# Low parts of the gated branches made by GpSimd and VectorE in turns

## Chip, cores and metric

The kernel runs on one core of a Trainium2 chip. The metric is the device time of one execution, in microseconds (us).

The engines are named as in the profile: PE is TensorE (PEld its weight loads), DVE is VectorE, ACT is ScalarE, POOL is GpSimd, SP issues most of the DMAs.

## The reference

Two layers of a diffusion trunk with two parallel token mixers: neighbourhood attention (branch a) and grouped-query attention (branch b), over 512 latent tokens and 256 context tokens of width 1024. What matters here is the end of a layer. The attention output of each branch is multiplied by the SiLU of its own gate path, projected to width 1024, merged by sigmoid gates, and projected once more:

```python
def _merge(a_att, b_att, a_z, b_z, g_a, g_b, w_o_a, w_o_b, w_out):
    o_a = (a_att * jax.nn.silu(a_z)) @ w_o_a      # width 512 -> 1024
    o_b = (b_att * jax.nn.silu(b_z)) @ w_o_b
    merged = jax.nn.sigmoid(g_a) * o_a + jax.nn.sigmoid(g_b) * o_b
    return merged @ w_out

# _layer:
out_x = _merge(a_att, b_att, a_z, b_z, g_a, g_b, w_o_a, w_o_b, w_out)
x_new = x + gate_x * out_x
```

Layer 0 does this for the context tokens too (768 columns in all), layer 1 for the latent tokens alone (512 columns). Everything is float32.

## The kernel before

**Split products.** A float32 matrix product is made of three matmuls (`mm3`, L435 to L437): both operands are split into a high part, rounded to the matmul's input type, and a low part, the rest; the three are high by high (L435), one with the low part of the activations or weights (L436), and the other (L437). Making a high part is a cast on ACT, making a low part is a subtraction of two SBUF operands. For the weights of the output projections this is L420 and L422 (`load_w2`), for other weights L405 and L408. Their subtractions are shared out by `mix_lo`, which gives odd pieces to DVE and even ones to POOL.

**Gated branches.** The gated outputs of the two branches lie in `za` and `zb`, with channels on partitions: four blocks of 128 channels (f = 0 to 3), each 128 x 768 in layer 0 and 128 x 512 in layer 1. `hilo` makes their high parts (`gah`, `gbh`, casts on ACT, L665) and their low parts (`gal`, `gbl`, subtractions, L666). It is called in three places:
- `prepare()` for all four blocks of branch a. This is in the middle of the grouped-query attention, since the first output projection of branch a (`o_chunks("a", ...)`) is one of the pieces of work with which that stage fills TensorE.
- `early()` for blocks 0 to 2 of branch b, at the end of the grouped-query attention.
- After the attention's pools are closed, block 3 of branch b, with DVE named as the engine.

**Work around them.** In the grouped-query stage each head has four query blocks. For each, TensorE makes scores (`pss`, L884 and L885), DVE subtracts the maximum (L1147), ACT takes the exponential (L1148), DVE or POOL makes the low half of the fp16 split (L836) before the transposing DMA, and TensorE forms the values (L1164, L1165). `divide` (L845 to L848) takes the reciprocal of the row sums, lets TensorE transpose it (L847, into `pst` or `psv`) and multiplies it into `zb` (L848). `head_out` adds the two halves of the value product (ACT L822, DVE L823) and multiplies them into `zb` (L827, on POOL mostly). The queries of the next heads are staged by L878. The context queries of layer 0 have a shorter path (L897, L899, L903).

**The psf bank.** The scores have two PSUM tiles in this stage, and the projections that fill it have one bank, `psf`: one group of twelve matmuls (four blocks by three) must be evicted (L701, DVE, which multiplies by the gate held in `tg`) before the next group may start.

**Order.** The program is not scheduled by hand: a scheduler with a timeline of its own sorts the instructions of each engine into one queue, which the engine then runs in order. An edit of one instruction's engine thus moves others.

The function edited and its callers:

Of the kernel before, what the change touches and what calls it, by code (L numbers as in the profile page):

```python
# [12 lines left out]
ALU = mybir.AluOpType  # L13
# [39 lines left out]
def R(ap):  # L53
    return ap.bitcast(F32R)
# [18 lines left out]
def hybrid_kernel(es: ExitStack, tc, x, ctx, cvec, w_ada, w_ada0, small, gvec, w_in, w_o_a, w_o_b, w_out,  # L73
                  bias_int, bias_edge, rope, ident_d, out):
    nc = tc.nc
    V, S, G, T = nc.vector, nc.scalar, nc.gpsimd, nc.tensor
# [351 lines left out]
    mix_lo = lambda k: V if k % 2 == 1 else G  # L428
# [164 lines left out]
    def layer(l, hx, nxt, start):  # L593
        first = l == 0
        ntok = NTOK if first else NLAT
# [62 lines left out]
        def hilo_tiles(name):  # L658
            return [big(name + part).rearrange("p (f n) -> p f n", f=4) for part in "hl"]

        def hilo(src, dst, fs, lo_eng=G, parts=((0, ntok),)):
            sv = src.rearrange("p (f n) -> p f n", f=4)
            for n0, n1 in parts:
                for f in fs:
                    S.copy(R(dst[0][:, f, n0:n1]), sv[:, f, n0:n1])  # L665
                    lo_eng.tensor_tensor(R(dst[1][:, f, n0:n1]), sv[:, f, n0:n1], dst[0][:, f, n0:n1], ALU.subtract)  # L666

        def load_tg(c):
            nc.sync.dma_start(tg[c].rearrange("p (f n) -> p f n", f=4)[:, :, :ntok], gs[c][:, :, :ntok])
# [18 lines left out]
        def prepare():  # L688

            gated["a"] = hilo_tiles("ga")  # L690
            hilo(za, gated["a"], range(4))
            for c in (0, 2):
                tg[c] = big("tg")
                load_tg(c)
# [90 lines left out]
        if True:  # L785
# [395 lines left out]
            def early():  # L1181

                for c in (1, 3):
                    tg[c] = big("tg")
                    load_tg(c)
                gated["b"] = hilo_tiles("gb")
                hilo(zb, gated["b"], range(3))
# [6 lines left out]
        with tc.tile_pool(name=f"mrg{l}", bufs=1, reuse_waits="tile") as mp:  # L1194
# [3 lines left out]
            for v in range(nv):  # L1198
                src = gd[l][8 * v:8 * v + 8].rearrange("k p -> (k p)").unsqueeze(0)
                nc.sync.dma_start(gv[:, v, :], src.to_broadcast([128, DM]))  # L1200
            hilo(zb, gated["b"], [3], V, spans)
            mg = []

# [312 lines left out]
```

## Time and profile before

| | |
|---|---|
| time, median of 3 runs | 1115.7 us (1115.24 to 1117.81) |
| time of the profiled execution | 1117.27 us |
| its span, first to last instruction | 1115.5 us |
| mean granted TensorE clock | 0.991 |
| busy: PE / DVE / ACT / POOL | 97% / 69% / 55% / 42% |
| L666 on POOL | 8 for branch a, 6 for branch b |
| L666 on DVE | 3, all of block 3 of branch b |

A profile line of the timeline reads: start, duration (both us), engine, line, operation, output tile <- input tiles, shape of output and input, count, and in brackets the idle time ahead of it with what ended it. A line of the waits reads: who waited <- for whom: us in total, times, longest. Where several like instructions follow each other they stand in one row with their count and the time from the first start to the last end.

### The profile page before, as it was taken

Reading aid. Unit: us, or ns where it says so; the run is one execution under the profiler, and the core shown is the slowest. Engines: PE = TensorE matmul, PEld = TensorE weight load, DVE = VectorE, ACT = ScalarE, POOL = GpSimd, SP = SyncE. Lnnn points to the kernel's source line nnn. Section 1 sums busy time; section 2 is a strip of 40 time slices with the busy share of each in tenths; the row PEclk is TensorE's granted clock in tenths of the full one; section 3 lists DMA queues with packets and bytes.
Section 4 is the critical chain, followed back from the end, with each engine's and each line's share of the span. In section 5 each row is a group of like instructions: output and inputs, shape, how many; then the busy total and the mean of one; then the engine's idle time right before and its main releaser. Section 6 shows DMA issues by size and latency. Waiting matters only on the chain. (4 is left out here: it accounts for less than half of the span.)

```text
span 1115.5 us, 16945 instructions
## 1 busy us (share of the span) xinstructions
PE 1077.0 (97%) x5672; PEld 878.7 (79%) x5672; DVE 764.8 (69%) x1600; ACT 617.7 (55%) x1236; POOL 468.2 (42%) x397
## 2 busy tenths in 40 slices
PE   8999999899999999869999999999999899999998
PEld 5688888788888877757788788888877888777677
DVE  4667799974378478676577785467997565677473
ACT  6454279776333576655330284445898446776430
POOL 1054235554246245454421445232446373564531
PEclk9999999999999999979999999999999999999999
DMA  9455324554543597869524542453565436879642
GB/s 370 143 171 151 90 70 115 123 137 121 174 145 110 140 207 172 171 197 261 181 89 133 181 128 79 138 161 98 129 148 133 145 99 169 198 226 238 192 150 78
DMA packets 236000, 171.79 MB, mean 154 GB/s; under 512 B 160140, under 2 KB 201864, under 8 KB 234248
## 3 DMA queue, kind: packets, MB, share of 16 engines
q1 hardware_dynamic: 228576, 156.31, 51.4%
q0 software_dynamic: 2368, 7.87, 2.2%
q10 hardware_dynamic: 4968, 6.53, 1.7%
q8 instruction: 45, 0.74, 0.3%
q14 instruction: 43, 0.35, 0.1%
HBM read 115.58 MB, written 17.32 MB: 119 GB/s over the span
## 5 line engine op out<-in xcount | busy, mean ns | idle before, releaser
L836 POOL TENSOR_TENSOR h<-p,h 128x256 f16<-128x256 f32 (+2 forms) x104 | 113.0, 1095 | 169.0 <-ACT h L835 121.1
L422 POOL TENSOR_TENSOR wlo<-raw,whi 128x512 fp32r<-128x512 f32 x70 | 98.6, 1413 | 124.4 <-ACT whi L420 81.4
L435 PE MATMUL psf<-hx,whi 128*128 128x512 f32 (+1 forms) x360 | 137.5, 382 | 2.5 <-ACT zt L623 1.3
L437 PE MATMUL psf<-hx,wlo 128*128 128x512 f32 (+1 forms) x360 | 135.5, 376 | 0.0
L436 PE MATMUL psf<-hx,whi 128*128 128x512 f32 (+1 forms) x360 | 135.3, 376 | 0.0
L435 PE MATMUL psx<-whi,hx 128*128 128x512 f32 (+1 forms) x328 | 121.0, 372 | 0.0
L420 ACT CAST whi<-raw 128x512 fp32r<-128x512 f32 x136 | 82.9, 620 | 67.9 <-DMA raw<-in_w_in_dram 41.7
L437 PE MATMUL psx<-whi,hx 128*128 128x512 f32 (+1 forms) x328 | 120.0, 367 | 0.0
L436 PE MATMUL psx<-wlo,hx 128*128 128x512 f32 (+1 forms) x328 | 119.6, 366 | 0.0
L405 ACT CAST whi<-raw 128x512 fp32r<-128x512 f32 x88 | 54.4, 623 | 103.9 <-PE psx L437 34.2
L408 POOL TENSOR_TENSOR wlo<-raw,whi 128x512 fp32r<-128x512 f32 x40 | 59.6, 1493 | 122.0 <-ACT whi L405 78.9
L506 POOL TENSOR_TENSOR ss<-ss,ehalf 128x8 f32<-128x8 f32 (+2 forms) x40 | 62.8, 1572 | 82.3 <-DVE ss L503 77.0
L422 DVE TENSOR_TENSOR wlo<-raw,whi 128x512 fp32r<-128x512 f32 x66 | 69.5, 1053 | 35.0 <-ACT whi L420 33.6
L835 ACT CAST h<-p 128x256 f16<-128x256 f32 (+2 forms) x136 | 81.6, 616 | 6.9 <-DMA ct<-h 3.4
L435 PEld LDWEIGHTS psf<-hx,whi 128*128 128x128 f32 x360 | 67.8, 188 | 15.1 <-ACT zt L623 2.4
L1147 DVE CUSTOM_DVE_ANT_0 p<-pss,vb 128x768 f32<-128x768 f32 x64 | 60.3, 953 | 25.7 <-PE pss L885 23.2
L1148 ACT ACTIVATE p<-pss,mx 128x768 f32<-128x768 f32 x64 | 57.6, 900 | 35.8 <-DVE mx L1147 34.9
L437 PEld LDWEIGHTS psf<-hx,wlo 128*128 128x128 f32 x360 | 67.8, 188 | 11.7
L436 PEld LDWEIGHTS psf<-hx,whi 128*128 128x128 f32 x360 | 67.9, 189 | 10.8
L437 PEld LDWEIGHTS psx<-whi,hx 128*128 128x128 f32 x328 | 61.9, 189 | 10.3
L436 PEld LDWEIGHTS psx<-wlo,hx 128*128 128x128 f32 x328 | 62.0, 189 | 9.4
L435 PEld LDWEIGHTS psx<-whi,hx 128*128 128x128 f32 x328 | 61.8, 189 | 9.1 <-issue 0.2
(338 smaller groups left out, 2975.5 us busy)
## 6 DMA issues: line engine op xcount, KB each, us to landing
raw<-in_w_in_dram SPq DMA_DIRECT2D x168, 256.0 KB, 3.0
rawb<-in_w_ada_dram SPq DMA_DIRECT2D x48, 256.0 KB, 2.7
raw<-in_w_out_dram SPq DMA_DIRECT2D x32, 256.0 KB, 2.9
tg<-gs SPq DMA_DIRECT2D x4, 1536.0 KB, 7.1
rawx<-in_w_ada_dram SPq DMA_DIRECT2D x4, 1024.0 KB, 9.8
rawy<-in_w_ada_dram SPq DMA_DIRECT2D x4, 1024.0 KB, 9.8
gs<-zt ACTq DMA_DIRECT2D x16, 256.0 KB, 2.8
raw<-in_w_o_a_dram SPq DMA_DIRECT2D x16, 256.0 KB, 3.2
```

Source lines behind the costliest of these rows:

```text
L405: S.copy(hi[:, :n], raw[:, :n])
L408: e.tensor_tensor(lo[:, :n], raw[:, :n], F(hi[:, :n]), ALU.subtract)
L420: S.copy(hi, raw)
L422: lo_eng(i).tensor_tensor(lo, raw, F(hi), ALU.subtract)
L435: T.matmul(ps, lhs[0], rhs[0], start=first, stop=False)
L436: T.matmul(ps, lhs[0], rhs[1], start=False, stop=False)
L437: T.matmul(ps, lhs[1], rhs[0], start=False, stop=last)
L506: G.tensor_tensor(ss, ss, ehalf[:, :n], ALU.pow)
L835: S.copy(h[:, 0], p[:, :n])
L836: eng.tensor_tensor(h[:, 1], p[:, :n], h[:, 0], ALU.subtract)
L1147: V.tensor_tensor_reduce(p, pss, lift, -1.0, 3e38, ALU.add, ALU.min, mx[:, 0:1])
L1148: S.activation(p, pss, AF.Exp, bias=mx[:, 0:1], accum_out=r[:, i:i + 1])
```

## The change

The default engine of `hilo` is no longer GpSimd. Where no engine is named, block f goes to the engine that `mix_lo` gives for it: blocks 1 and 3 to VectorE, blocks 0 and 2 to GpSimd. The call that names VectorE is not touched. So in each layer f = 1 and 3 of branch a and f = 1 of branch b move to VectorE.

```diff
-        def hilo(src, dst, fs, lo_eng=G, parts=((0, ntok),)):
+        def hilo(src, dst, fs, lo_eng=None, parts=((0, ntok),)):
             sv = src.rearrange("p (f n) -> p f n", f=4)
             for n0, n1 in parts:
                 for f in fs:
                     S.copy(R(dst[0][:, f, n0:n1]), sv[:, f, n0:n1])
-                    lo_eng.tensor_tensor(R(dst[1][:, f, n0:n1]), sv[:, f, n0:n1], dst[0][:, f, n0:n1], ALU.subtract)
+                    (lo_eng or mix_lo(f)).tensor_tensor(R(dst[1][:, f, n0:n1]), sv[:, f, n0:n1], dst[0][:, f, n0:n1], ALU.subtract)
```

The order of the queues changes with it. First VectorE in layer 0, where branch a is prepared; `gal` is the low part, `wlo` a weight's low part, `qs` the staged queries, `mx` and `p` the softmax's. Before:

```order
L897 TENSOR_REDUCE mx_5427<-pss_5422 128x2
L899 TENSOR_SCALAR mx_5427<-mx_5427 128x2
L1147 ISA p_5553,mx_5554<-pss_5548,vb_3419 128x768
L1147 ISA mx_5554 128x1
L848 TENSOR_SCALAR zb_4067<-pst_5616,vb_3419,zb_4067 64x512
L422 TENSOR_TENSOR wlo_5499<-raw_5495,whi_5497 128x512
L878 TENSOR_TENSOR qs_5721<-qb_3734,qs_5721 64x768
L845 RECIPROCAL r_5431<-r_5431 128x2
L823 TENSOR_TENSOR ho_5471<-psv_5462,ho_5471 64x256
```

And now:

```order
L897 TENSOR_REDUCE mx_5427<-pss_5422 128x2
L666 TENSOR_TENSOR gal_5309<-za_1053,gah_5308 128x768
L899 TENSOR_SCALAR mx_5427<-mx_5427 128x2
L848 TENSOR_SCALAR zb_4067<-pst_5616,vb_3419,zb_4067 64x512
L1147 ISA p_5553,mx_5554<-pss_5548,vb_3419 128x768
L1147 ISA mx_5554 128x1
L666 TENSOR_TENSOR gal_5309<-za_1053,gah_5308 128x768
L422 TENSOR_TENSOR wlo_5499<-raw_5495,whi_5497 128x512
L878 TENSOR_TENSOR qs_5721<-qb_3734,qs_5721 64x768
L823 TENSOR_TENSOR ho_5471<-psv_5462,ho_5471 64x256
L845 RECIPROCAL r_5431<-r_5431 128x2
```

Two low parts stand ahead of L422 and of L823, the first (f = 1) also ahead of L899; on GpSimd four in a row have become two at the same place.

TensorE at the same place, where `psf_5322` is the first group of the projection of branch a and `psv_5640` the transposed reciprocals. Before:

```order
L435 MATMUL psf_5322<-gah_5308,whi_5053 128x512
L884 MATMUL pss_5561<-gk_3421,qs_5543 128x512
L885 MATMUL pss_5561<-gk_3421,qs_5543 128x512
L884 MATMUL pss_5561<-gk_3421,qs_5543 128x256
L885 MATMUL pss_5561<-gk_3421,qs_5543 128x256
L847 MATMUL psv_5640<-ident,r_5431 128x128 x2
L884 MATMUL pss_5574<-gk_3421,qs_5543 128x512
```

And now:

```order
L436 MATMUL psf_5322<-gal_5309,whi_5053 128x512
L437 MATMUL psf_5322<-gah_5308,wlo_5055 128x512
L435 MATMUL psf_5322<-gah_5308,whi_5059 128x512
L884 MATMUL pss_5561<-gk_3421,qs_5543 128x512
L885 MATMUL pss_5561<-gk_3421,qs_5543 128x512
L884 MATMUL pss_5561<-gk_3421,qs_5543 128x256
L885 MATMUL pss_5561<-gk_3421,qs_5543 128x256
L884 MATMUL pss_5574<-gk_3421,qs_5543 128x512
L885 MATMUL pss_5574<-gk_3421,qs_5543 128x512
L884 MATMUL pss_5574<-gk_3421,qs_5543 128x256
L885 MATMUL pss_5574<-gk_3421,qs_5543 128x256
L847 MATMUL psv_5640<-ident,r_5431 128x128 x2
```

Three more matmuls of the group (with block 1's low part) and the second score group have moved ahead of L847; the rest of `psf_5322` stands behind it and is now followed by the next group, `psf_5336`, without scores between.

VectorE in layer 1, where branch b is prepared; `psf_10927` is the group of branch a's projection whose eviction (L701) frees the psf bank:

```order
 L823 TENSOR_TENSOR ho_10895<-pst_10882,ho_10895 64x512
+L666 TENSOR_TENSOR gbl_10946<-zb_9765,gbh_10945 128x512
 L701 TENSOR_SCALAR tg_10560<-tg_10560,psf_10927 128x512
 L848 TENSOR_SCALAR zb_9765<-pst_10953,vb_9238,zb_9765 64x512
 L422 TENSOR_TENSOR wlo_11106<-raw_11102,whi_11104 128x512
+L408 TENSOR_TENSOR wlo_11194<-raw_11190,whi_11192 128x512
 L823 TENSOR_TENSOR ho_10973<-pst_10960,ho_10973 64x512
 L827 TENSOR_TENSOR zb_9765<-zb_9765,ho_10973 64x512
-L408 TENSOR_TENSOR wlo_11194<-raw_11190,whi_11192 128x512
 L666 TENSOR_TENSOR gbl_10946<-zb_9765,gbh_10945 128x512
```

Block 1's low part has come between L823 and the eviction L701; the last L666, of block 3, was on VectorE before too. In the same layer the two low parts of branch a go behind L836 and ahead of an L1147, and elsewhere in layer 0 weights' low parts and SP's loads change places with their neighbours.

## The prediction

> **What bounds the kernel now.** I read the page first, then the windows, TensorE's waits, and the timelines of the places where the changed instructions stand.
>
> ```profile
> PE 1077.0 (97%) x5672; PEld 878.7 (79%) x5672; DVE 764.8 (69%) x1600; ACT 617.7 (55%) x1236; POOL 468.2 (42%) x397
> PEclk9999999999999999979999999999999999999999
> ```
>
> TensorE is busy for 97% of the span. An edit on VectorE or GpSimd can therefore win only TensorE's idle gaps and the time in which its clock is lowered, and it loses whatever new gap it makes. The slices show one weak place, the 18th of forty (474 to 502 us), where the granted clock drops to 7 tenths. The windows give its size (start:end, length, then the busy time of each engine, clock, DMA share, GB/s):
>
> ```profile
> 480.00:500.00 20.00, 11.63 (x53) 9.30 (x52) 16.20 (x14) 10.77 (x21) 14.29 (x10) 0.68 0.69 213
> ```
>
> TensorE is busy for 11.63 of 20 us there, at a clock of 0.68. The waits of TensorE name what ended its gaps; the first three rows are of 470 to 640 us (layer 0), the last two of 980 to 1115 us (layer 1):
>
> ```profile
> PE psv L847 <- DVE ho L823: 6.2, 1, 6.2
> PE psf L435 <- ACT zt L623: 1.6, 1, 1.6
> PE psf L436 <- POOL gal L666: 0.6, 1, 0.6
> ...
> PE psf L436 <- POOL wlo L408: 1.7, 1, 1.7
> PE psf L436 <- POOL gbl L666: 1.1, 1, 1.1
> ```
>
> The low parts that are edited (L666) show up as 0.6 and 1.1 us. The 6.2 us stand in VectorE's name, and its timeline shows that this too goes back to L666 on GpSimd. GpSimd first, then VectorE:
>
> ```profile
> 482.29 1.29 POOL L827 TENSOR_TENSOR zb<-zb,ho 64x512 f32<-64x512 f32 x1
> 483.54 1.27 POOL L422 TENSOR_TENSOR wlo<-raw,whi 128x512 fp32r<-128x512 f32 x1
> 484.77 7.14 POOL L666 TENSOR_TENSOR gal<-za,gah 128x768 fp32r<-128x768 f32 x4
> 491.86 1.27 POOL L422 TENSOR_TENSOR wlo<-raw,whi 128x512 fp32r<-128x512 f32 x1
> ```
>
> ```profile
> 483.12 0.56 DVE L899 TENSOR_SCALAR mx<-mx 128x2 f32<-128x2 f32 x1
> 483.67 0.96 DVE L1147 CUSTOM_DVE_ANT_0 p<-pss,vb 128x768 f32<-128x768 f32 x1
> ...
> 484.67 0.76 DVE L848 SCALAR_TENSOR_TENSOR zb<-pst,vb,zb 64x512 f32<-64x512 f32 x1
> 485.45 8.22 DVE L422 TENSOR_TENSOR wlo<-raw,whi 128x512 fp32r<-128x512 f32 x1
> 493.71 0.95 DVE L878 TENSOR_TENSOR qs<-qb,qs 64x768 fp32r<-64x768 f32 x1
> 494.69 0.17 DVE L845 RECIPROCAL r<-r 128x2 f32<-128x2 f32 x1
> 494.89 0.42 DVE L823 TENSOR_TENSOR ho<-psv,ho 64x256 f32<-64x256 f32 x1
> ```
>
> VectorE's subtraction L422, two operands in SBUF, took 8.22 us and ended just after GpSimd's last instruction did (491.86 + 1.27 = 493.13). It did nothing for five GpSimd instructions. Behind it in VectorE's queue stood L823, which frees the bank into which TensorE's L847 writes:
>
> ```profile
> 486.64 0.50 PE L436 MATMUL psf<-gal,whi 128*128 128x512 f32 x1 [0.58 <-POOL gal L666]
> ...
> 487.69 0.63 PE L884 MATMUL pss<-gk,qs 128*128 128x512 f32 x1
> 488.12 0.63 PE L885 MATMUL pss<-gk,qs 128*128 128x512 f32 x1
> ...
> 495.36 0.69 PE L847 MATMUL psv<-ident,r 128*128 128x128 f32 x2 [6.19 <-DVE ho L823]
> ...
> 497.98 0.63 PE L435 MATMUL psf<-gah,whi 128*128 128x512 f32 x1
> 498.41 0.63 PE L436 MATMUL psf<-gal,whi 128*128 128x512 f32 x1
> ...
> 500.89 0.39 PE L885 MATMUL pss<-gk,qs 128*128 128x512 f32 x1
> ...
> 1042.65 0.40 PE L435 MATMUL psf<-gbh,whi 128*128 128x512 f32 x1
> 1042.88 0.39 PE L436 MATMUL psx<-gbl,whi 128*128 128x512 f32 x1
> ```
>
> The starts of neighbouring 128x512 matmuls are 0.43 us apart at 487.69 and at 497.98, and 0.23 at 1042.65: half rate from before the long wait until past 498.4. At 500.89 a matmul takes 0.39 us again. The gaps of 1.6 and 0.6 us, the second of which ended at 486.64, are all that stands in the rows ahead of it. [...]
>
> **The change part by part.** Six of the fourteen low parts that GpSimd makes go to VectorE, three in each layer.
>
> ```profile
> L666 POOL TENSOR_TENSOR gal<-za,gah x8: 1269/1762/1832, 484.8 to 994.7; 128x768 fp32r<-128x768 f32 x4, 128x512 fp32r<-128x512 f32 x4
> L666 DVE TENSOR_TENSOR gbl<-zb,gbh x3: 426/684/1754, 546.4 to 1054.0; 128x512 fp32r<-128x512 f32 x2, 128x256 fp32r<-128x256 f32 x1
> ...
> 543.71 2.23 DVE L422 TENSOR_TENSOR wlo<-raw,whi 128x512 fp32r<-128x512 f32 x1
> ...
> 543.09 6.80 POOL L666 TENSOR_TENSOR gbl<-zb,gbh 128x768 fp32r<-128x768 f32 x3
> ```
>
> A 128x768 low costs GpSimd 7.14 / 4 = 1.79 us, and VectorE 0.95 by the 64x768 subtraction at 493.71 (as many elements for each partition). A 128x512 low takes VectorE 0.68. GpSimd loses about 3 x 1.8 + 3 x 1.4 = 9.6 us (1.4 lies between the row's least, 1.27, and its median), and VectorE gains 3 x 0.95 + 3 x 0.68 = 4.9. Neither sum is on the path: both engines are idle for a third of the span or more. What counts is when the lows come and what waits behind them.
>
> How long VectorE waits for GpSimd is the open price. At 543.71 it got its turn after some 1.6 us of waiting (2.23 less 0.68), one GpSimd instruction; at 485.45 only after five. [...] By one instruction the layer-0 gain would be the larger of the two below; the row at 485.45, with five, contradicts it.
>
> *Layer 0, branch a.* VectorE's low of f = 1 now stands before L899, that of f = 3 after L1147; GpSimd does f = 0 and 2. TensorE does seven psf matmuls and both score groups before L847, where it did four and one. I compare at one point of equal work: before, TensorE had done L847, both score groups and seven psf matmuls at 498.41.
> - Turns after each instruction: VectorE's f = 1 runs 483.58 to 484.5 behind L827; L422 and f = 0 on GpSimd end at 485.8 and 487.6; L899, L848 and L1147 (first inputs in PSUM or 2 columns) fill VectorE to 486.4; f = 3 to 488.55, GpSimd's f = 2 to 490.35, then L422 (0.66), GpSimd's L422 (1.27), L878 (0.95) and L823 (0.42), L845 (0.17): 493.9. L847 goes at 494.0 and takes 0.35: equal work at 494.35, a gain of 4.05. Half rate then lasts longer after that point than before: 2.4 us of it were left (to the 500.8 of the row at full rate), now up to 6.45; half of the difference is lost, 0 to 2.0. With 1.15: gain 2.9.
> - Starved again: GpSimd's L422, f = 0, f = 2 and L422 end at 489.6; then VectorE's f = 1, L899, L848, L1147, f = 3, L422, L878, L823, L845 need 0.95 + 0.1 + 0.76 + 0.96 + 0.95 + 0.66 + 0.95 + 0.42 + 0.17 = 5.9: L847 at 495.6, equal work at 495.95, gain 2.45, less 0.6 of half rate: 1.9.
> I take 2.9; it is nearest to the handing over at 543.71, and the bounds are 0 (all as before) and 7.4 (rival A).
>
> *Layer 0, after it.* Two psf groups now follow each other with no scores between, through a single psf bank. The second waits for a whole eviction: L701 is 0.69 us for 512 columns, plus a hand-over. Rows:
>
> ```profile
> 548.22 0.69 DVE L701 SCALAR_TENSOR_TENSOR tg<-tg,psf 128x512 f32<-128x512 f32 x1
> ...
> 1036.00 0.50 PE L435 MATMUL psf<-gah,whi 128*128 128x512 f32 x1 [0.17 <-DVE tg L701]
> ```
>
> Cost 0.69 + 0.17 = 0.85 (0 if VectorE is early, 2 if it is once more held for one GpSimd low). w_out's lows and SP's loads also shift among each other; no row prices that. The 1.7 us at L408 above are the largest wait of TensorE on a weight's low in these stretches, so the bounds are 0 and 1.7, and below nothing -1.7 if that wait should go. Taken at +0.3, since TensorE's wait on SP's loads shows in none of the five rows.
>
> *Layer 1.*
>
> ```profile
> 993.00 0.96 DVE L1147 CUSTOM_DVE_ANT_0 p<-pss,vb 128x768 f32<-128x768 f32 x1 [1.89 <-PE pss L885]
> ...
> 1039.21 0.67 DVE L823 TENSOR_TENSOR ho<-pst,ho 64x512 f32<-64x512 f32 x1
> ...
> 1038.69 2.11 POOL L836 TENSOR_TENSOR h<-p,h 128x768 f16<-128x768 f32 x1
> 1040.76 4.21 POOL L666 TENSOR_TENSOR gbl<-zb,gbh 128x512 fp32r<-128x512 f32 x3
> ...
> 1042.08 0.50 PE L436 MATMUL psf<-gbl,whi 128*128 128x512 f32 x1 [1.05 <-POOL gbl L666]
> ```
>
> Branch a's two lows stand ahead of L1147 at 993.00, which VectorE awaited idle for 1.89 us; 2 x 0.68 fits in, with one turn of waiting each it is late by up to 1.6. Softmax work hides it mostly: +0.3, bounds 0 and 1.6. Branch b's f = 1 stands behind L823 (over at 1039.88) and ahead of L701, which frees the psf bank for TensorE. It waits for GpSimd's L836 (1040.80), runs to 1041.5, L701 to 1042.2; GpSimd's f = 0 starts at 1041.5 and ends at 1042.9. TensorE's L436 goes at 1042.95 where it went at 1042.08: +0.85.
>
> Sum: -2.9 + 0.85 + 0.3 + 0.3 + 0.85 = -0.6 us. The profiled execution took 1117.27 us (span 1115.5 and 1.8 around it), 1.57 above the median of the runs. So 1116.7 by its own time, and 1115.7 - 0.6 = 1115.1 against the median.
>
> **Rivals.** A measurement of this kernel tells some 0.3% from no change, 3.35 us: below 1112.35 is faster, above 1119.05 slower.
> [...]
> - B, slower: branch b's f = 1 in layer 1 starves. GpSimd runs L836, f = 0 and f = 2 without a pause, to 1040.80 + 2 x 1.4 = 1043.6. If VectorE is held until then, or through the weight low behind it (1.3), f = 1 ends at 1044.3 to 1045.6 and L701 frees the bank at 1045.0 to 1046.3: TensorE stands for 4.5 us or more. L436 at 1045.3 is +3.2, and a clock halved for some 5 us adds 2.5: 5.7 in place of 0.85, net +4.25: 1119.95. It decides if f = 1 starts after 1043. For it: 485.45. Against it: the two hand-overs in the rows above, 2.23 at 543.71 and the 1754 ns of an L666 on VectorE.
> - C, nothing moves: VectorE's f = 1 in layer 0 starves so long that L847 goes as late as before, and the event gains 0. Then -0 + 2.3: 1118.0, within 0.3%.
>
> **How the numbers follow.** Forecast 0.33 (its own range, 1112.5 to 1117.7, from the event's 1.9 to 5.2 and the small terms), A 0.24, B 0.25, C 0.18. Faster: most of A and a little of the forecast's, 0.26. Slower: B's larger part, the upper end of C with w_out's 1.7, 0.30. Same: 0.44. The range runs from A, 1110.6 less the 1.7 of L408's wait, 1109, to B with its longer hold (+1.3), 1121.
>
> **What would show it.** Right: VectorE's L422 of 8.22 us is gone or under 3, L847's wait falls from 6.19 to under 4, the windows row of 480:500 has a clock over 0.68, and L666 stands with x2 on GpSimd at both places of each layer. The term for layer 1 is right if TensorE's psf gap after 1040 is 2 to 2.5 us in all. Wrong: a VectorE subtraction of over 4 us at either place (C or B), psf waits on L701 of over 2 us in sum in layer 0, or a total of TensorE's gaps and half rate that differs from before by over 3 us at places where no low was moved.

## The result and the profile after

The changed kernel took 1128.2 us (median of 5 runs, 1125.1 to 1129.0) against 1116.9 before (5 runs): a ratio of 1.0097, 95% interval 1.0085 to 1.0109, or 10.8 us slower by the ratio (the medians lie 11.3 apart). Forecast were 1115.1 us, in a range of 1109 to 1121.

The profiled execution took 1126.65 us, with a span of 1124.9. Its page, in the rows that answer to those of before:

```profile
PE 1079.6 (96%) x5672; PEld 880.5 (78%) x5672; DVE 770.4 (68%) x1606; ACT 617.7 (55%) x1236; POOL 462.4 (41%) x391
```

GpSimd has lost 5.8 us of busy time, VectorE gained 5.6, and TensorE runs the same 5672 matmuls. So the loss lies in when things happen. TensorE's timeline around the long wait of before:

```profile
483.48 0.50 PE L435 MATMUL psf<-gah,whi 128*128 128x512 f32 x1 [1.60 <-ACT zt L623]
...
485.31 0.80 PE L436 MATMUL psf<-gal,whi 128*128 128x512 f32 x1 [1.33 <-POOL gal L666]
...
489.99 0.50 PE L884 MATMUL pss<-gk,qs 128*128 128x512 f32 x1 [0.78 <-ACT p L1148]
491.88 0.43 PE L847 MATMUL psv<-ident,r 128*128 128x128 f32 x2 [0.93 <-DVE r L845]
494.85 0.39 PE L435 MATMUL psf<-gah,whi 128*128 128x256 f32 x1 [1.38 <-DVE tg L701]
```

The wait of 6.19 us at L847 is 0.93 now: the stall that the prediction built on is gone. It did not go the way that was forecast, though. VectorE and GpSimd at that place:

```profile
480.92 1.45 DVE L666 TENSOR_TENSOR gal<-za,gah 128x768 fp32r<-128x768 f32 x1
482.30 4.77 DVE L899 TENSOR_SCALAR mx<-mx 128x2 f32<-128x2 f32 x1
...
481.46 2.04 POOL L422 TENSOR_TENSOR wlo<-raw,whi 128x512 fp32r<-128x512 f32 x1
483.46 3.58 POOL L666 TENSOR_TENSOR gal<-za,gah 128x768 fp32r<-128x768 f32 x2
```

The first low had its turn after some 0.5 us. But the instruction behind it, two columns wide and 0.56 us long before, stood for 4.77 us, while GpSimd ran a weight's low and its two branch lows. The hold had moved to another instruction.

What was lost is seen elsewhere. TensorE's waits between 500 and 730 us of the changed kernel (before, this stretch had 1.2 on L701, 0.9 on y, and nothing else above 0.3):

```profile
PE psf L435 <- DVE tg L701: 3.3, 3, 2.7
PE pst L343 <- ACT half L346: 1.8, 2, 1.0
PE pst L1164 <- issue: 1.7, 1, 1.7
PE pss L884 <- ACT p L903: 1.6, 1, 1.6
PE psx L436 <- POOL wlo L408: 1.3, 1, 1.3
```

The largest, 2.7 us, is at branch b's lows of layer 0. VectorE there, the TensorE row that it ends, and GpSimd:

```profile
532.85 2.58 DVE L666 TENSOR_TENSOR gbl<-zb,gbh 128x768 fp32r<-128x768 f32 x1
535.46 0.70 DVE L823 TENSOR_TENSOR ho<-pst,ho 64x512 f32<-64x512 f32 x1
536.19 0.42 DVE L701 SCALAR_TENSOR_TENSOR tg<-tg,psf 128x256 f32<-128x256 f32 x1
...
536.66 0.80 PE L435 MATMUL psf<-gah,whi 128*128 128x512 f32 x1 [2.67 <-DVE tg L701]
...
532.64 4.45 POOL L666 TENSOR_TENSOR gbl<-zb,gbh 128x768 fp32r<-128x768 f32 x2 [1.84 <-PE psv L919]
```

A low of 0.95 us took 2.58 while GpSimd was making its two; the eviction of the single psf bank stood behind it, and TensorE behind the eviction. (Not all of the 2.67 us is that low's: experiment 1 has 1.54 us at the same eviction without it.)

To see where the 9.4 us between the two spans arise, I count TensorE's work: each matmul counts with its time at full rate, and for each moment of before I take the time at which the changed kernel had started as much work. The total work is the same to the last digit (1043.8 us), so this lag is time won (-) or lost (+), gaps and half rate together. Increase of the lag, us, by stretch of before's time:

| stretch (us) | what runs there | after | before + earlier L297 (control) |
|---|---|---|---|
| 0-460 | nothing that was edited | -2.1 | -1.5 |
| 460-503 | layer 0, branch a's lows, the long wait | -3.5 | -0.3 |
| 503-565 | layer 0, rest of attention, branch b's lows | +4.8 | +0.1 |
| 565-635 | merge, first part of w_out | -0.2 | +1.6 |
| 635-672 | end of layer 0, start of layer 1 | +5.7 | -0.9 |
| 672-985 | layer 1 up to branch a's lows; order as before | +1.7 | +0.9 |
| 985-1012 | layer 1, branch a's lows | +2.6 | -0.4 |
| 1012-1062 | layer 1, branch b's lows | +0.3 | -0.2 |
| 1062-1108 | tail | 0.0 | 0.0 |

Two kernels with the same code in a stretch differ there by up to 2 us (the first row, the sixth, and in some runs the last), so there only differences above that are read. In the stretches that are read below, kernels without an edit that reaches them differ by 0.8 us at most.

### The profile page after: what moved, and what is told of

It reads as the page before. It is cut to its first block, busy times and chain, and to the rows that moved or that the text cites. A ratio compares the mean times of both kernels' runs of the same rounds, so it can differ in the third digit from the quotient of the medians.

```text
span 1124.9 us, 16945 instructions
## 1 busy us (share of the span) xinstructions
PE 1079.6 (96%) x5672; PEld 880.5 (78%) x5672; DVE 770.4 (68%) x1606; ACT 617.7 (55%) x1236; POOL 462.4 (41%) x391
## 3 DMA queue, kind: packets, MB, share of 16 engines
q10 hardware_dynamic: 4968, 6.53, 1.8%
## 5 line engine op out<-in xcount | busy, mean ns | idle before, releaser
L836 POOL TENSOR_TENSOR h<-p,h 128x256 f16<-128x256 f32 (+2 forms) x104 | 113.7, 1101 | 165.6 <-ACT h L835 118.0
L422 POOL TENSOR_TENSOR wlo<-raw,whi 128x512 fp32r<-128x512 f32 x70 | 99.5, 1426 | 132.7 <-ACT whi L420 81.7
L435 PE MATMUL psf<-hx,whi 128*128 128x512 f32 (+1 forms) x360 | 137.5, 382 | 2.4 <-ACT zt L623 1.2
L436 PE MATMUL psf<-hx,whi 128*128 128x512 f32 (+1 forms) x360 | 135.4, 376 | 0.0
L435 PE MATMUL psx<-whi,hx 128*128 128x512 f32 (+1 forms) x328 | 122.3, 375 | 0.0
L436 PE MATMUL psx<-wlo,hx 128*128 128x512 f32 (+1 forms) x328 | 120.9, 369 | 1.4 <-POOL wlo L408 1.3
L408 POOL TENSOR_TENSOR wlo<-raw,whi 128x512 fp32r<-128x512 f32 x40 | 60.3, 1513 | 128.7 <-ACT whi L405 93.0
L405 ACT CAST whi<-raw 128x512 fp32r<-128x512 f32 x88 | 54.9, 626 | 93.3 <-DMA raw<-in_w_in_dram 34.3
L422 DVE TENSOR_TENSOR wlo<-raw,whi 128x512 fp32r<-128x512 f32 x66 | 61.8, 936 | 39.7 <-ACT whi L420 38.4
L435 PEld LDWEIGHTS psf<-hx,whi 128*128 128x128 f32 x360 | 67.8, 188 | 15.0 <-ACT zt L623 2.3
L1147 DVE CUSTOM_DVE_ANT_0 p<-pss,vb 128x768 f32<-128x768 f32 x64 | 60.3, 953 | 23.5 <-PE pss L885 20.7
L436 PEld LDWEIGHTS psf<-hx,whi 128*128 128x128 f32 x360 | 67.9, 189 | 10.8
L436 PEld LDWEIGHTS psx<-wlo,hx 128*128 128x128 f32 x328 | 62.4, 190 | 11.7 <-POOL wlo L408 2.4
L435 PEld LDWEIGHTS psx<-whi,hx 128*128 128x128 f32 x328 | 62.3, 191 | 9.3 <-issue 0.2
```

The source lines that it names most:

```text
L405: S.copy(hi[:, :n], raw[:, :n])
L408: e.tensor_tensor(lo[:, :n], raw[:, :n], F(hi[:, :n]), ALU.subtract)
L422: lo_eng(i).tensor_tensor(lo, raw, F(hi), ALU.subtract)
L435: T.matmul(ps, lhs[0], rhs[0], start=first, stop=False)
L436: T.matmul(ps, lhs[0], rhs[1], start=False, stop=False)
L836: eng.tensor_tensor(h[:, 1], p[:, :n], h[:, 0], ALU.subtract)
```

## The experiments

The ratios are against runs of the kernel before on the same chip, with 5 rounds each.

**1 to 4: one call in one layer at a time.** The edit names the engine again in all calls but one; here branch a of layer 0, the others likewise:

```diff
-            hilo(za, gated["a"], range(4))
+            hilo(za, gated["a"], range(4), None if first else G)
...
-                hilo(zb, gated["b"], range(3))
+                hilo(zb, gated["b"], range(3), G)
```

Expected, in the order branch a of layer 0, branch b of layer 0, branch a of layer 1, branch b of layer 1:

> Only branch a's lows of layer 0 alternate; all other lows stay on GpSimd. Theory 1 (two causes in layer 0): the stall at L847 is shortened as in the changed kernel, 3.5 us won by 505, but the queues' new order lets the first token of w_out end some 34 matmuls later, so that the chain of L297 for layer 1's modulation starts 7 us later and costs 5.8 between 646 and 667: +1 to +4 us in all, with the gap at 534 (L701) gone. Rival (the lows themselves cost, by contention with GpSimd, and the order is harmless): -3.5 us and no late L297.

> Only branch b's f = 1 of layer 0 goes to VectorE. Theory 1: the stall of 6.2 us at L847 stays, the low is held for more than 2 us by GpSimd's two and L701 with it, TensorE waits about 2.5 us and runs at half rate after it: +2 to +5 us; the L297 chain starts as before and the stretch of 646 to 667 costs nothing. Rival (order is harmless, lows cost): about +10 us, all the loss of layer 0 being branch b's.

> Only branch a's lows of layer 1 alternate. TensorE's order is that of the kernel before. Theory 1: a gap of 1.9 us in front of a psf group (L435 for L701) where it was 0.5, and half rate after it: +2.6 us as in the changed kernel. Rival (that gap comes from the shift of the work ahead of it, not from the lows): under +0.5.

> Only branch b's f = 1 of layer 1 goes to VectorE, ahead of L701. Theory 1: the gap of 1.05 us at L436 turns into one of 1.4 at L435: +0.3 us. Rival (the low starves behind GpSimd's two, as the prediction's case B has it): a gap of over 4 us, +5.7 us.

| lows that alternate | ratio (95%) | lag 460-503 | 503-565 | 635-672 | 985-1012 |
|---|---|---|---|---|---|
| a, layer 0 | 1.0038 (1.0024 to 1.0053) | -3.4 | +3.3 | +6.0 | -0.3 |
| b, layer 0 | 1.0055 (1.0038 to 1.0071) | -0.1 | +3.9 | +4.1 | -0.2 |
| a, layer 1 | 1.0030 (1.0021 to 1.0040) | 0.0 | -0.1 | +0.1 | +2.6 |
| b, layer 1 | 1.0000 (0.9989 to 1.0010) | -0.2 | -0.1 | +0.2 | -0.3 |

Branch a of layer 0 wins its 3.4 us and loses them, and more, in stretches without a low of branch a: the rival, in which the order is harmless, falls. Its time, 4.2 us above before, lies just over the expected +1 to +4, and the gap at L701 that was to go is still there. TensorE's longest waits between 503 and 565 in that run, where blocks 0 to 2 of branch b are made by GpSimd as before:

```profile
511.63 0.50 PE L884 MATMUL pss<-gk,qs 128*128 128x512 f32 x1 [1.56 <-ACT p L903]
533.54 0.38 PE L1164 MATMUL pst<-ht,vb 128*128 128x512 f16 x1 [2.48 <-issue]
539.71 0.50 PE L435 MATMUL psf<-gah,whi 128*128 128x512 f32 x1 [1.54 <-DVE tg L701]
```

So +3.3 us of this stretch come with branch a's edit alone, through a wait on the softmax (L903), one that the profile gives no cause for ("issue"), and one on L701 with no low of branch b ahead of it on VectorE. The changed kernel has the first two as well (1.6 and 1.7). No run shows which shift of the order makes them.

Branch b of layer 0 lies above its expected +2 to +5: it too loses 4.1 us between 635 and 672, which theory 1 had excluded. Its local part was as expected. VectorE, GpSimd and TensorE:

```profile
543.35 2.50 DVE L666 TENSOR_TENSOR gbl<-zb,gbh 128x768 fp32r<-128x768 f32 x1
545.77 2.28 DVE L422 TENSOR_TENSOR wlo<-raw,whi 128x512 fp32r<-128x512 f32 x1
548.09 0.43 DVE L823 TENSOR_TENSOR ho<-psv,ho 64x256 f32<-64x256 f32 x1
...
542.73 4.77 POOL L666 TENSOR_TENSOR gbl<-zb,gbh 128x768 fp32r<-128x768 f32 x2
...
548.57 0.80 PE L460 MATMUL psx<-gbh,whi 128*128 128x512 f32 x1 [2.77 <-DVE ho L823]
```

A low and a weight's low on VectorE take 4.70 us from start to end, about as long as two lows on GpSimd (4.77). L823, which TensorE awaits, starts 6.53 us after the L701 ahead of it (541.56), where in the kernel before it was 4.05 (541.92 and 545.97): 2.5 us later. From 549.16 to 551.30 TensorE's matmuls of 128x512 start 0.43 us apart, half rate. GpSimd loses little: in the kernel before its three lows took 6.80 us here, 2.27 each.

In layer 1, branch a costs 2.6 us by itself. VectorE, GpSimd and TensorE of that run:

```profile
992.75 3.22 DVE L666 TENSOR_TENSOR gal<-za,gah 128x512 fp32r<-128x512 f32 x2 [0.18 <-ACT gah L665]
996.01 0.96 DVE L1147 CUSTOM_DVE_ANT_0 p<-pss,vb 128x768 f32<-128x768 f32 x1
...
1001.42 2.08 DVE L836 TENSOR_TENSOR h<-p,h 128x768 f16<-128x768 f32 x1 [0.16 <-ACT h L835]
1003.53 0.69 DVE L701 SCALAR_TENSOR_TENSOR tg<-tg,psf 128x512 f32<-128x512 f32 x1
...
992.28 3.15 POOL L666 TENSOR_TENSOR gal<-za,gah 128x512 fp32r<-128x512 f32 x2 [0.52 <-ACT gah L665]
...
1004.27 0.49 PE L435 MATMUL psf<-gah,whi 128*128 128x512 f32 x1 [1.93 <-DVE tg L701]
...
1006.33 0.63 PE L436 MATMUL psf<-gal,whi 128*128 128x512 f32 x1
```

The pair takes 3.22 us for 1.36 of work. L701 is on the way from there to TensorE: it is late by 1.5 us, the gap in front of psf is 1.93 where it was 0.47, and matmuls take 0.63 us soon after: half rate. Branch b of layer 1 costs nothing: its low took 1.54 us, one hand-over, and the gap of 1.05 us at L436 became one of 1.35 at L435.

**5: all four lows of branch a, layer 1, on VectorE.** TensorE's order is the same as before, and the four stand where the two stood.

```diff
+            hilo(za, gated["a"], range(4), G if first else V)
```

> All four of branch a's lows of layer 1 go to VectorE at the place where the two stood; TensorE's order is that of the kernel before. With two lows the pair took 3.22 us for 1.36 of work, and L1147, L836 and L701 behind it came 1.5 us late. Lock theory (VectorE loses its time to GpSimd's lows, which run at the same moment): four lows without GpSimd beside them take 2.7 to 3.3 us, and L836 behind them is no longer stretched to 2 us; the gap in front of the psf group falls from 1.9 towards 0.5, the time to that of the kernel before +-1. Queue theory (each low on VectorE delays what stands behind it, contention or not): worse than with two lows, +5 us or more.

The ratio was 1.0018 (1.0005 to 1.0030); the lag of 985-1012 rose by 0.4 us, where two lows had cost 2.6.

```profile
988.94 2.48 DVE L666 TENSOR_TENSOR gal<-za,gah 128x512 fp32r<-128x512 f32 x4
991.45 0.96 DVE L1147 CUSTOM_DVE_ANT_0 p<-pss,vb 128x768 f32<-128x768 f32 x1
...
997.18 2.09 DVE L836 TENSOR_TENSOR h<-p,h 128x768 f16<-128x768 f32 x1 [0.16 <-ACT h L835]
```

Four lows alone, with GpSimd idle, take 2.48 us, less than two beside GpSimd's. So in this place contention, not VectorE's own work, delays what stands behind the lows. Not as expected: L836 stays at 2.09 us, while GpSimd's L827 and L836 run, and the gap in front of psf is 1.26 us, not 0.5. The whole time is 2 us above before, which this stretch does not show; the profiled execution took 1113.84 us, 4.0 less than the median of this kernel's runs. The intervals of the two ratios, with two lows and with four, overlap, so that contention is the cost rests on the traces.

**6: four buffers for the L297 chain.** Between 635 and 672 the changed kernel waits for the modulation of layer 1: a chain of 32 L297 (two for each of 16 tiles of w_ada), which runs as background work beside the first pass of w_out, a few steps after each token. In the changed kernel w_out's first token ends 34 matmuls later in TensorE's queue, and the chain starts behind it. It ends with L306; that row before, the same after, and the wait of ScalarE on what follows from it (L242) after:

```profile
643.17 0.19 DVE L306 TENSOR_TENSOR as<-asum 128x32 f32<-128x32 f32 x1
...
650.14 0.19 DVE L306 TENSOR_TENSOR as<-asum 128x32 f32<-128x32 f32 x1
...
ACT half L346 <- DVE modc L242: 2.1, 1, 2.1
```

TensorE's 1.8 us on L346 stand behind that wait. The edit gives the chain's tiles four buffers:

```diff
-            cb["w"] = pool.tile([128, 512], F32, tag="rawb", name=nm("rawb"), bufs=2)
+            cb["w"] = pool.tile([128, 512], F32, tag="rawb", name=nm("rawb"), bufs=4 if queue else 2)
```

In the kernel before, and with branch a of layer 0 alternating:

> Control: the kernel before, with four buffers in place of two for the tiles of the L297 chain that runs beside w_out of layer 0. Late-chain theory: the chain is not what TensorE waits for here, so within 1.5 us of the kernel before. Rival (the chain already costs time before): faster by 2 us or more.

> Branch a's lows of layer 0 alternate, and the L297 chain has four buffers. Late-chain theory: the chain's pace was set by two tiles in flight; with four it ends well before 643 however late it starts, the gaps at L343 and L408 near 655 and the half rate after them go (5.8 us), and what is left is the gain at L847 and the small losses of 505 to 547: about -1 us against the kernel before. Rival (the 5.8 us come from w_in's weights or from ACT, not from the chain): still +4 us.

The control gave 0.9998 (0.9987 to 1.0010), as expected. With branch a it was 1.0033 (1.0017 to 1.0048): 3.7 us slower than before, hardly better than without the buffers. The chain did end in time:

```profile
639.59 0.19 DVE L306 TENSOR_TENSOR as<-asum 128x32 f32<-128x32 f32 x1
```

and still 2.5 us were lost between 635 and 672, in waits of TensorE on w_in's weights (0.92 on L405, 0.43 on L408) and on L346. ScalarE, which casts the weights, had a long wait of its own there (its waits from 638 to 675):

```profile
ACT whi L405 <- DMA raw<-in_w_in_dram: 3.7, 1, 3.7
```

So this expectation failed: a chain in time is not enough. The order of w_in's loads and casts moves with the rest, and TensorE's waits point at it.

**7, 8, 9: the chain starts earlier.** Its first six steps stand ahead of w_out's first token; two of the three tiles that they read have long been loaded.

```diff
-            run(bg, 1)
+            run(bg, 7)
```

With branch a of layer 0; in the changed kernel, all else alternating; and in the kernel before:

> Branch a's lows of layer 0 alternate, and the first six steps of the L297 chain are put ahead of w_out's first token instead of behind it. Late-chain theory: the chain starts with its two tiles that have been loaded since 540 and ends 5 us or more sooner; the loss of 5.8 us falls to under 2, -1 to +1 us in all. Rival (not the chain): still +4 us.

> The changed kernel with the first six steps of the L297 chain ahead of w_out's first token, and nothing else. Late-chain theory: the 5.8 us of 646 to 667 fall to under 1.5, and the sum of the other parts is left: +5 to +7 us against the kernel before (the changed kernel: about +11). Rival (the chain's share is that of branch a alone and another wait takes its place when both branches alternate): +9 or more.

> Control: the kernel before with the first six steps of the L297 chain ahead of w_out's first token. Late-chain theory: the chain is in time in the kernel before, so nothing is won but the gap of 0.9 at 640: 0 to -1.5 us. Rival (the edit wins time in any kernel, and the best version owes its gain to it): -3 us or more.

| kernel with the earlier start | ratio (95%) | lag 635-672 | without it |
|---|---|---|---|
| a, layer 0 | 0.9998 (0.9982 to 1.0014) | +0.7 | +6.0 |
| changed kernel | 1.0051 (1.0036 to 1.0065) | -1.1 | +5.7 |
| before | 1.0008 (0.9999 to 1.0017) | -0.9 | 0 |

TensorE's busy time, first column after the length, of 640 to 680 us in the changed kernel, then with the earlier start:

```profile
640.00:680.00 40.00, 36.84 (x170) 28.97 (x169) 30.25 (x56) 24.31 (x60) 14.52 (x17) 0.96 0.40 124
```

```profile
640.00:680.00 40.00, 40.00 (x200) 33.21 (x199) 31.71 (x57) 27.83 (x68) 14.72 (x17) 1.00 0.36 114
```

The loss of this stretch is gone where the lows' engines alternate, and nothing is won in the kernel before (+0.9 us by the ratio, where 0 to -1.5 was expected). So some 5 of the changed kernel's 10.8 us come with the order around w_out, and not with a wait for a low.

That the late chain is the whole way from the order to the loss is not shown. With branch b alone ScalarE does not wait for L242 at all; with the earlier start in the changed kernel it does, for 2.6 us, and TensorE loses nothing. Counted at equal work, the chain ends some 8.5 us later than before in the changed kernel and with branch a alone (lost: 5.7 and 6.0), and 2.4 us later with branch b alone, whose first token ends only 3 matmuls later (lost: 4.1). It ends under 1 us later both in the changed kernel with the earlier start, which loses nothing, and with four buffers, which still lose 2.5. The earlier start moves w_in's loads too, and no run keeps the two apart.

**10: branch b of layer 0, with the earlier start.**

> Only branch b's f = 1 of layer 0 on VectorE, with the first six steps of the L297 chain ahead of w_out's first token. Late-chain theory: the loss of 4.3 us between 642 and 675 goes, the local one (2.4 at L823 and 1.5 of half rate) stays: +2.5 to +4.5 us. Rival (the later loss is independent of the chain): still +6 or more.

1.0038 (1.0024 to 1.0051), 4.2 us: within the expected, and the lag fell by 1.1 between 635 and 672. Left are the +3.9 of 503 to 565, which in experiment 2 are gap and half rate.

**11: three lows of branch b, layer 0, on VectorE.**

```diff
+                hilo(zb, gated["b"], range(3), V if first else G)
```

> Branch b's f = 0 to 2 of layer 0 all go to VectorE. With f = 1 alone on VectorE that low took 2.50 and the L422 behind it 2.28, both held by GpSimd's lows, and TensorE waited 2.8 us. Lock theory: three lows take about 2.9 us on VectorE without a hold, L422 runs in 0.7, so the gap is no larger than 2 us and the time +0 to +4. Queue theory: three lows ahead of L823 and L701 are worse than one: +7 or more.

The ratio was 1.0062 (1.0050 to 1.0074), 6.9 us and outside of the lock theory's +0 to +4. Yet the place itself was as that theory has it:

```profile
542.98 2.70 DVE L666 TENSOR_TENSOR gbl<-zb,gbh 128x768 fp32r<-128x768 f32 x3
545.59 0.68 DVE L422 TENSOR_TENSOR wlo<-raw,whi 128x512 fp32r<-128x512 f32 x1
```

Three lows take 2.70 us, one beside GpSimd took 2.50; the gap fell from 2.77 to 0.67 us and the lag of 503-565 rose by 0.6 only. The loss is of 635 to 672 (+4.7): each kernel with layer 0's lows moved and no earlier chain loses there.

**12 and 13: all four lows of branch a, layer 0, on VectorE, without and with the earlier chain.**

```diff
+            hilo(za, gated["a"], range(4), V if first else G)
```

> All four of branch a's lows of layer 0 go to VectorE, and none runs on GpSimd beside them. Lock theory: they take some 4 x 0.95 = 3.8 us unless GpSimd's L422 is in the way, no VectorE instruction there is held for over 2 us (8.22 before, 4.77 with the alternating lows), and 4 us or more are won at L847. The order of w_out's tokens lies between the two kernels (the first token ends 16 matmuls later than before, not 34), so the late chain should cost 1 to 4 us: -3 to +1 us in all. Queue theory (VectorE's own work is the cost): the gain at L847 is smaller than the 3.5 us of the alternating lows.

> The same, with the first six steps of the L297 chain ahead of w_out's first token. If both theories hold (lock in the attention stage, late chain behind it), the gain at L847 stays and the loss of 646 to 667 is under 1 us: -5 to -2 us against the kernel before, and the only version that beats it. If either is wrong, within 1 us of the kernel before or slower.

Without: 1.0002 (0.9991 to 1.0014). The stretch of 460-503 won 5.9 us, more than with two lows; one of the four took 3.27 us beside GpSimd's weight lows, so it was held for over the 2 us that I had set as the limit. Two of VectorE's four lows, and GpSimd:

```profile
483.61 4.63 DVE L666 TENSOR_TENSOR gal<-za,gah 128x768 fp32r<-128x768 f32 x2
...
484.18 3.24 POOL L422 TENSOR_TENSOR wlo<-raw,whi 128x512 fp32r<-128x512 f32 x2
```

The stretch of 503-565 took 1.0 back, that of 635-672 2.9. With the earlier chain: 0.9967 (0.9957 to 0.9977), 1112.8 us, 3.7 us faster than before and within the expected. It is the only version here that beats both kernels. Here 503-565 takes 4.0 us back instead of 1.0, and 635-672 nothing; why the first grew is not shown.

## Why the prediction was wrong

**The long wait at L847 (-2.9 forecast): the size was near, the path another, so in part luck.** Forecast was that VectorE and GpSimd take turns after each instruction, with L899, L848 and L1147 free to run in between. Measured: f = 1 did wait for one instruction, but then the two-column L899 was the one held, once for three GpSimd instructions (4.77 us), and after it f = 3 and L422 ran free (0.95 and 0.68 us, GpSimd having finished). That L848 and L1147 are free was an estimate from the kernel before, where they took 0.76 and 0.96 us beside GpSimd's L422 and L666; in the changed kernel they took as long. The start of the psf group, the same work in both traces, puts the two beside each other; then the point of equal work that the prediction names:

```profile
485.56 0.49 PE L435 MATMUL psf<-gah,whi 128*128 128x512 f32 x1 [1.60 <-ACT zt L623]
...
492.07 0.48 PE L436 MATMUL psf<-gal,whi 128*128 128x512 f32 x1
```

The first row is of before and answers to 483.48 of after, 2.08 us earlier; the second is of after and answers to 498.41 of before. So L847 went at 491.88 + 2.08 = 493.96, forecast 494.0, and the gain at equal work was 498.41 - 492.07 - 2.08 = 4.26 us, forecast 4.05. The half rate then had the other sign: forecast were 1.15 us of loss, but the changed kernel was back at full rate by then and won some 0.9 more (the next matmuls of 128x512 start 0.23 us apart, 0.43 before). From this went the wait of 1.38 us on L701 between the two psf groups, the term that was forecast at +0.85. The stretch came to -3.5, where -2.9 + 0.85 = -2.05 was forecast.

**The rest of layer 0: wrong, the step that decided.** The failing sentence is "w_out's lows and SP's loads also shift among each other ... Taken at +0.3", together with what the sum has no term for: branch b's low in layer 0. Beside that L701 term, 0.3 us were forecast for all of layer 0 after the long wait; measured were 4.8 between 503 and 565 and 5.7 between 635 and 672.
- Branch b's low ahead of L701 was priced in layer 1 only. VectorE's new order had the same low in layer 0 ahead of L823 and L701, and there it is longer (128x768) and was held: by itself it cost 3.9 us, gap and half rate together (experiments 2 and 10). That is rival B's mechanism, in the other layer. It is not the whole of the 4.8: branch a's edit alone costs 3.3 in the same stretch, and the two do not add up.
- The shift around w_out was bounded by one wait of before, 1.7 us, which is one of layer 1; neither of the two windows of waits that the prediction read (470 to 640 and 980 to 1115) has the stretch of 640 to 672 in it. The new order ended w_out's first token 34 matmuls and the L297 chain 7 us later. Experiments 7 and 8 take the 5 to 7 us of this stretch away again by an earlier start of that chain. Whether the chain itself or w_in's loads and casts made TensorE wait stays open.

**Layer 1, branch a (+0.3 forecast): mis-sized.** Measured +2.6 (experiment 3). "Softmax work hides it mostly" did not hold: L701 stood behind that softmax work in VectorE's queue, so the 1.5 us of delay reached TensorE whole, and half rate followed (0.43 us apart from 1005.90).

**Layer 1, branch b (+0.85): the mechanism right, the size too high.** The low waited for one GpSimd instruction, as forecast (1.53 us). The psf gap after 1040 was 1.39 us in place of 1.05, not the 2 to 2.5 that were to show the term right: +0.3, and a ratio of 1.0000. Rival B did not come about here.

**The signs.** Those of being right came for the long wait (L422 0.68 us, L847's wait 0.93, L666 with x2 on GpSimd at both places of each layer, and a clock of 0.91 from 480 to 500), yet they say nothing of the rest. Of those of being wrong two came: waits on L701 of 4.7 us in layer 0, and a loss of over 3 us between 635 and 672, where no low was moved.

**The chances.** Slower had 0.30. The sum by the measured terms is -3.5 + 4.8 - 0.2 + 5.7 + 2.6 + 0.3 = +9.7; the rows with no edit in them (-2.1 and +1.7) nearly cancel. No run shows the 7.4 us of rival A, on which its 1110.6 and the low end of the range, 1109, rest: the gain at equal work was 4.26 us, and the stretch of 460-503 won 3.5 us here and 5.9 in experiment 12; TensorE started matmuls of 128x512 0.43 us apart from 485.90, after gaps of 1.60 and 1.33 us, and 0.23 apart from 488.58. Two terms were each taken at 0.3, near their low end, because the trace of before showed little waiting there.

## What to carry to other kernels

When the edit reorders the queues of a scheduled kernel, follow what has moved, each chain with its length and each group of loads, to the point where TensorE needs its end; the waits of the old trace did not bound it here. Sharing work between VectorE and GpSimd at the same moment can cost more VectorE time than giving it all to VectorE: two lows took 3.22 us (experiment 3), four 2.48 (experiment 5). For each instruction put into a queue, name the next one behind it that frees a single buffer (here L701), in each layer.

## What the runs showed of the hardware

A VectorE instruction of two columns, L899, 0.13 to 1.42 us long in the kernel before, was held for 4.77 us in the changed kernel while GpSimd's subtractions ran back to back (481.46 to 487.04). GpSimd was slowed too: in the changed kernel its L422 took 2.04 us beside VectorE's first low, the next L422 1.27 us. Which engine gave way differed from place to place: VectorE's low got its turn after one GpSimd instruction in layer 1 (1.54 us, experiment 4), and took 3.27 us beside weight lows in experiment 12. What decides it stays open.

Half rate was seen again after short gaps: after the single gap of 1.93 us at layer 1's psf (experiment 3), matmuls of 128x512 started 0.43 us apart from 1005.90 to 1008.46. After single gaps of 1.26 us (experiment 5), 1.35 us (experiment 4) and 1.39 us (the changed kernel in layer 1) they went on 0.23 us apart.
